# Half of the activations turned by VectorE's 32 x 32 blocks instead of by TensorE, in a one-core hybrid decoder step

## The chip, the cores and the metric

The kernel runs on one core of a Trainium2 chip. The metric is device time in microseconds of one execution, the median of several runs. TensorE (PE) does matmuls and, by an identity matrix, transposes; VectorE (DVE) and ScalarE (ACT) work on data elementwise; GpSimd (POOL) does small copies; SyncE (SP) issues DMAs. POOL and ACT can issue DMAs too, each on a queue of its own.

## The reference

One layer of a decoder, for a prompt of 256 tokens and 8 x 4 sample tokens that share the weights. Each token's row x of 2048 features goes through one wide projection, a gated short convolution (A), a gated DeltaNet (B), a merge with sigmoid gates, an output projection with layer norm, and a feed-forward part with a second layer norm:

```python
proj = x @ w_in
gB, gC, h, q, k, v, z, b_logit, a_logit, m_a, m_b = jnp.split(proj, split_points, axis=-1)
conv_out, new_conv_a = causal_depthwise_conv(gC * h, conv_a_buf, conv_a_w)
y_a = (gB * conv_out) @ w_a_out
qkv, new_gdn_buf = causal_depthwise_conv(jnp.concatenate([q, k, v], -1), gdn_buf, gdn_conv_w)
...
o, S = gated_delta_rule(qh, kh, vh, g, beta, S0)
...
y_b = o @ w_b_out
merged = jax.nn.sigmoid(m_a) * y_a + jax.nn.sigmoid(m_b) * y_b
x = layer_norm(ALPHA * x + merged @ w_o, ln1_g, ln1_b)
x = layer_norm(ALPHA * x + jnp.square(jax.nn.relu(x @ w_up)) @ w_down, ln2_g, ln2_b)
```

All inputs and outputs are float32. The outputs are both token sets, the convolution histories and the delta-rule states.

## The kernel before, in words

**Data layout.** Features lie on partitions and tokens along the free axis: `xh` and `xl` are [128, 16, 288], sixteen feature tiles by 256 prompt and 32 sample tokens. Every float32 operand is split in two: `xh` is x rounded to the matmul format, `xl` the rest, and each weight block likewise into `hi` (a cast on ACT, line 188) and `lo` (a subtraction on DVE, line 143). A product is then three matmuls: hi by xh, hi by xl (line 220) and lo by xh (line 222).

**Blocks.** All weights are cut into blocks of 512 KB, kept in a list `blocks`. One loop runs over them; the order of its statements is the order of the work on each engine, since the program is scheduled by hand. In step i it does the splits of a block two or three ahead, the evacuations that are due (`due`), the matmuls of block i, and the load of block i+6 or i+7 (`load`, SP's queue). `raw`, `hi` and `lo` have four buffers each, so a load waits until the `lo` subtraction of the block four earlier has read the buffer. A block has 24 matmuls of 288 columns; `fill` is a list of small jobs that are slipped into PE's stream, one after each lo matmul (line 223).

**The first eight blocks.** Blocks 0 to 3 need only the first eight feature tiles of x (two tiles each, 512 columns of the k and q projections). Blocks 4 and 5 need feature tiles 8 to 11, blocks 6 and 7 tiles 12 to 15.

**How x gets there.** `xr[i]` (i = 0 to 3) receives 512 features of the 256 prompt tokens, tokens on partitions, rows of 2 KB, and `xs4` the sample tokens. PE turns each 128 x 128 piece (line 942 for the prompt, line 926 for the sample); ACT casts the result from PSUM into `xh`, DVE subtracts to `xl`. For i = 0 this is done ahead of the loop and inside block 0; for i = 1, 2, 3 `x_fill(i)` puts nine transposes (eight and one) into `fill` in blocks 1, 3 and 5.

**Other early loads.** `later_loads` issues `xr[3]`, its sample part and then seven small loads on SP: the convolution histories and weights (`hwr`, `har`) and the norm parameters (`lnr`). PE turns these in block 6 (`hist_tiles`, `hist_tiles2`, lines 968 to 977). The four entries of `rest` load the constants `cf` and `cfe`, the 16 columns of w_in for beta and the decay (`wbar`), and `ci` and `arow`; they are issued at the ends of blocks 2 to 5. `gates`, a generator that runs from block 8 on, copies `wbar` (line 992), adds `xh` and `xl`, and multiplies them (line 1001, in block 13).

**Start of SP's queue.** x tile 0 and the weights of block 0 in pieces, block 1, `xr[1]`, its sample part, blocks 2 and 3, `xr[2]`, its sample part, block 4, then `later_loads`, then block 5.

Of the kernel before, what the change touches and what calls it, by code (L numbers as in the profile page):

```python
# [9 lines left out]
F32 = mybir.dt.float32  # L10
# [6 lines left out]
P = 128  # L17
D = 2048
NP_ = 256
NS = 32  # L20
NT = NP_ + NS
# [85 lines left out]
def hybrid_kernel(ctx: ExitStack, tc: tile.TileContext, A):  # L107
# [31 lines left out]
    act, dve, pe, gps, sp = nc.scalar, nc.vector, nc.tensor, nc.gpsimd, nc.sync  # L139


    def tt(out, a, b, op):
        dve.tensor_tensor(out=out, in0=a, in1=b, op=op)  # L143
# [4 lines left out]
    MUL, ADD, SUB, MIN, MAX = ALU.mult, ALU.add, ALU.subtract, ALU.min, ALU.max  # L148
# [19 lines left out]
    def load(i, steps=(), between=()):  # L168
        if i >= len(blocks):
            return  # L170
        gi, r0, k0, _, _ = blocks[i]
        t = wp.tile([P, KB, GW], F32, tag="raw", name=nm("raw"))
        kb, cols = gi["kb"], gi["cols"]
        dst = t.rearrange("p k c -> p (k c)").rearrange("p (k c) -> p k c", k=kb)
        src = gi["W"][r0:r0 + kb * P, gi["col0"]:gi["col0"] + cols].rearrange("(k p) c -> p k c", p=P)
        k = 0
        for step in steps or (kb,):
            sp.dma_start(dst[:, k:k + step], src[:, k:k + step])
            k += step
            if between:  # L180
                between.pop(0)()
        raw[i] = t
# [67 lines left out]
    xh = xp.tile([P, KT, NT], F32R, tag="XH", name="xh")  # L250
    xl = xp.tile([P, KT, NT], F32R, tag="XL", name="xl")
# [3 lines left out]
    wbar = ao0[:, NL - NE:NL - NE + 16 * KT].rearrange("p (k c) -> p k c", c=16)  # L255
# [609 lines left out]
    tx = tx_cm.__enter__()  # L865
# [6 lines left out]
            pe.matmul(wps.rearrange("p (u c) -> p u c", u=4)[:, 0:u], warm, bmid(warm, u), start=True, stop=True)  # L872

    warm_up(5)
    xr = [tx.tile([P, 2, 512], F32, name=f"xr{i}") for i in range(4)]
    xs4 = tx.tile([P, 512], F32, name="xs4")
    xpr = A["x_prompt"][0].rearrange("(b p) f -> p b f", p=P)
    xsr = A["x_sample"].rearrange("b t (c j p) -> c (b t) j p", j=4, p=P)
    hwr = tx.tile([112, 768], F32, name="hwr")
# [7 lines left out]

    def x_sample_in(c, queue=sp):
        queue.dma_start(xs4[:, c * P:c * P + P], xsr[c])

    def w_first(k, a=0, b=2):
        sp.dma_start(raw[0][:, 2 * k + a:2 * k + b, :],
# [10 lines left out]
    x_sample_in(1)  # L903
    load(2)
    load(3)
    sp.dma_start(xr[2], xpr[:, :, 1024:1536])
    x_sample_in(2)
    gps.memset(epsc[:, 0:1], LN_EPS)
    gps.memset(epsc[:, 1:2], NORM_EPS)
    gps.memset(epsc[:, 2:3], 1.28e-10)  # L910

    def later_loads():
        sp.dma_start(xr[3], xpr[:, :, 1536:2048])
        x_sample_in(3)
        sp.dma_start(hwr[0:96, :], A["state_gdn_conv"][0].rearrange("b j (g c) -> (b j g) c", g=4))
        sp.dma_start(hwr[96:112, :], A["gdn_conv_w"][0].rearrange("j (g c) -> (j g) c", g=4))
        sp.dma_start(har[0:64, :], A["state_conv_a"][0].rearrange("b j (g c) -> (b j g) c", g=4))
        sp.dma_start(har[64:76, :], A["conv_a_w"][0].rearrange("j (g c) -> (j g) c", g=4))
        sp.dma_start(lnr[0:16, :], A["ln1_g"].rearrange("o (k p) -> (o k) p", p=P))
        sp.dma_start(lnr[16:32, :], A["ln1_b"].rearrange("o (k p) -> (o k) p", p=P))  # L920
        sp.dma_start(lnr[32:33, :], A["gdn_norm_w"])


    def x_sample(i):
# [30 lines left out]
    def x_fill(i):  # L955
        def step(u):
            def f():
                turns, out = x_steps(i)[u]()
                for g in turns + out:
                    g()  # L960
            return f
        return step(0), lambda: x_sample(i)(), step(1)

    def hist_tiles():
        g = gtile()
        hv = hw.rearrange("p (g u) c -> p u g c", u=6)
# [19 lines left out]
    def gates(first):  # L986
# [1 line left out]
        xs0 = gd["pool"].tile([P, 12 * NT + KT * 32], F32, tag="S0", name="xf0")  # L988
        xf = (xs0[:, 0:12 * NT].rearrange("p (k t) -> p k t", k=12), gd["pool"].tile([P, 4, NT], F32, tag="b4", name="xf1"))
        wba = xs0[:, 12 * NT:].rearrange("p (k c) -> p k c", k=KT)  # L990
        for u in range(2):
            act.copy(wba[:, :, 16 * u:16 * u + 16], wbar)
        for u in range(4):
            ks = slice(4 * u, 4 * u + 4)
            tt(xf[0][:, ks] if u < 3 else xf[1], xh[:, ks, 0:NT], xl[:, ks, 0:NT], ADD)
            yield
        yield
        gb = gtile()
        for k in range(KT):
# [550 lines left out]
    def side():  # L1550
        first = gdn(0)
        yield from gates(first)
        for G in range(2):
            while cur[0] < mark["kqv", G] + 20 or aux:
                yield
            yield from first if G == 0 else gdn(G)
            if G == 0:
                states_out(0, 24, 3, 27, "kdec", A["new_gdn_conv_prompt"][0, 0], A["new_gdn_conv_sample"][0])
# [45 lines left out]
                     sp.dma_start(arow[:, 0, :], A["a_log"].to_broadcast([P, 8])),  # L1604
                     sp.dma_start(arow[:, 1, :], A["dt_bias"].to_broadcast([P, 8])))]
    load(4)
    later_loads()
    load(5)
    sgen = side()
    gcm = None  # L1610
    for p in range(8):
# [2 lines left out]
    for i in range(len(blocks)):  # L1614
        cur[0] = i
        ahead = AHEAD if i > 9 else 2
        if i == 10:
            split_hi(i + 2)
            split_lo(i + 2)
        if i > 5:  # L1620
            split_hi(i + ahead)
        if i in (1, 3, 5):
            a_, s_, b_ = x_fill(i // 2 + 1)
            fill.extend([idle, a_, s_, b_])
        if i == 6:
            fill.extend([idle, idle, idle, idle, hist_tiles, hist_tiles2])
        if i == 7:
            tx_cm.__exit__(None, None, None)
            gcm = tc.tile_pool(name="gdn", bufs=1)
            gpool = gcm.__enter__()  # L1630
            gd["pool"] = gpool
            gd["w1"] = [gpool.tile([P, 640], F32, tag=f"w1{u}", name=f"w1{u}") for u in range(2)]
            for w in gd["w1"]:
                gps.memset(w[:, 0:3], 0.0)
            gps.memset(stBA, 0.0)
            for G in range(2):
                gd["kq", G] = gpool.tile([P, 4, 4, 2, 64], F32, tag="kq", name=f"kq{G}", bufs=2)
                gd["kqs", G] = gpool.tile([P, 2, 4, 8, 4], F32, tag="kqs", name=f"kqs{G}", bufs=2)
                gd["v", G] = gpool.tile([P, 2, 4, 2, 64], F32, tag="vf", name=f"vf{G}")
                gd["vs", G] = gpool.tile([P, 4, 8, 4], F32, tag="vfs", name=f"vfs{G}")  # L1640
        if i > 7 and sgen:
            if i == mark["merge"]:
                for _ in sgen:
                    pass
                sgen = None
            else:
                next(sgen, None)
                if aux and next(aux[0], aux) is aux:
                    aux.pop(0)
            if i == mark["z"] + 4:  # L1650
                states_out(24, 32, 2, 18, "vf", A["new_conv_a_prompt"][0, 0], A["new_conv_a_sample"][0])
            if i == mark["conv"] + 1:
                gd["ao"] = ap_.tile([P, 2, H, NT], F32, tag="ao", name="ao")
        late = i >= mark["end"] - 1
        if i > 5 and not late:
            split_lo(i + ahead)
        for f in due.pop(i, ()):
            f()
        if late:
            split_lo(i + ahead)  # L1660
        if i == mark["merge"]:
            gcm.__exit__(None, None, None)
            p3 = pool("p3")
            ph["pool"] = p3
            r1 = p3.tile([P, KT, NT], F32R, tag="R1", name="ahl")
            r4 = p3.tile([P, KT, NX], F32R, tag="R4", name="ohl")
            ph["mg"] = p3.tile([P, KT, NX], F32, tag="R3", name="mg")[:, :, 0:NT]

            def halves(key, r, src):
                for q in range(2):  # L1670
                    s = slice(4 * q, 4 * q + 4)
                    s8 = slice(8 + 4 * q, 12 + 4 * q)
                    act.copy(r[:, s, 0:NT], src[:, s, :])
                    tt(r[:, s8, 0:NT], src[:, s, :], r[:, s, 0:NT], SUB)
                ph[key + "h"], ph[key + "l"] = r[:, 0:8, :], r[:, 8:16, :]

            halves("a", r1, gd["ao"][:, 0])
            at(i + 9, lambda: halves("o", r4, gd["ao"][:, 1]))
        if i == mark["down3"]:
            tail_tiles()  # L1680
        if i == mark["down3"] - 60:
            tail_consts()
        if i == mark["end"] - 3:
            sample_sum()
        if i == mark["end"] - 1:
            sample_products()
        matmuls(i)
        if i < 6:
            for u, step in {0: ((1, 2),), 1: ((2, 1), (3, KB))}.get(i, ((i + 2, KB),)):
                split_hi(u, step)  # L1690
                split_lo(u, step)
        if i == 10:
            load(i + 6)
        load(i + ahead + 4)
        if 2 <= i < 6:
            rest[i - 2]()
    for i in sorted(due):
        for f in due[i]:
            f()
# [30 lines left out]
```

## Time and profile before

| | |
|---|---|
| median of 3 runs | 1661.1 us (1660.97 to 1662.16) |
| profiled execution | 1660.64 us, span 1658.7 us |
| granted TensorE clock, mean | 0.999 |
| PE busy | 1650.5 us (100% of the span), 13142 matmuls |
| DVE / ACT / POOL busy | 979.2 / 781.8 / 134.1 us |
| DMA | 280.47 MB, mean 169 GB/s |
| DMA busy share 10 to 20, 20 to 30, 30 to 40 us | 0.93, 1.03, 0.86 |

The span is what the profiler saw of the program; the time is what the run took with what lies around it. Rows of the timeline read: start in us, duration in us, engine, line of the kernel, operation, output<-input, shapes, count, and in brackets how long the engine had been idle and what ended that. SPq and POOLq are DMA issues on those queues. A row with a count above 1 merges neighbours, and its duration runs from the first start to the last end. In the DMA list the last number is the median time from issue to landing.

### The profile page before, as it was taken

The numbers are of one execution on the slowest core, as the hardware profiler recorded it, in microseconds if no ns is written. First come the engines' busy times: TensorE is split into PE (matmuls) and PEld (weight loads), VectorE is DVE, ScalarE is ACT, GpSimd is POOL, SyncE is SP. The second block draws the span as 40 slices with busy tenths as digits, with TensorE's granted clock in tenths as the row PEclk, the third lists the DMA queues.
The fourth block names the chain that finished last, engine by engine and source line by source line (L and its number), as shares of the span: only waits on it lengthen the run. The fifth ranks groups of instructions, "written<-read, shape, count | busy, mean of one in ns | idle before, by whom it ended". The sixth has DMA issues, their size and how long they took to land.

```text
span 1658.7 us, 31399 instructions
## 1 busy us (share of the span) xinstructions
PE 1650.5 (100%) x13142; PEld 1635.6 (99%) x13142; DVE 979.2 (59%) x1299; ACT 781.8 (47%) x1217; POOL 134.1 (8%) x259
## 2 busy tenths in 40 slices
PE   9999999999999999999999999999999999999998
PEld 8999999999999999999999999999999999999997
DVE  6788688767544444457776666444444444444466
ACT  6786756448533333334444455443334433344353
POOL 0142216133000000000000000000000000000011
PEclk9999999999999999999999999999999999999999
DMA  8555457645555555554565555555555555555552
GB/s 272 173 171 169 138 172 203 183 130 176 184 170 165 166 165 166 165 166 154 167 218 165 166 165 166 165 165 166 165 166 165 166 165 166 165 165 166 179 164 97
DMA packets 273251, 280.47 MB, mean 169 GB/s; under 512 B 13727, under 2 KB 267220, under 8 KB 272848
## 3 DMA queue, kind: packets, MB, share of 16 engines
q1 hardware_dynamic: 269334, 266.33, 51.5%
q0 software_dynamic: 3632, 12.08, 2.6%
q8 instruction: 103, 1.69, 0.4%
q14 instruction: 38, 0.31, 0.0%
q10 hardware_dynamic: 144, 0.07, 0.0%
HBM read 270.95 MB, written 7.48 MB: 168 GB/s over the span
## 4 chain that ended last, share of the span: by engine, by line
PE 98%; DVE 1%; ACT 1%; DMA 0%; issue 0%; SPq 0%; ACTq 0%
PE acc L220 62%; PE acc L222 31%; PE acc L725 1%; PE g L1297 0%; PE g L1469 0%; PE g L1489 0%; PE g L1492 0%; PE g L1288 0%; DMA xr<-in_x_prompt_dram 0%; PE g L1189 0%; PE g L1447 0%; DVE lo L143 0%; PE g L1481 0%; PE g L942 0%; DVE w L146 0%
## 5 line engine op out<-in xcount | busy, mean ns | idle before, releaser
L143 DVE TENSOR_TENSOR lo<-raw,hi 128x1024 fp32r<-128x1024 f32 (+1 forms) x503 | 607.4, 1210 | 582.1 <-ACT hi L188 579.2
L188 ACT CAST hi<-raw 128x1024 fp32r<-128x1024 f32 (+1 forms) x499 | 519.2, 1043 | 738.5 <-PE acc L220 654.9
L220 PE MATMUL acc<-xh,hi 128*128 128x288 f32 x1408 | 398.2, 298 | 0.3 <-ACT xh L931 0.2
L220 PE MATMUL acc<-xl,hi 128*128 128x288 f32 x1408 | 394.1, 295 | 0.1
L222 PE MATMUL acc<-xh,lo 128*128 128x288 f32 x1408 | 302.7, 296 | 0.3 <-DVE lo L143 0.3
L220 PE MATMUL acc<-dl,hi 128*128 128x288 f32 (+1 forms) x1024 | 287.7, 295 | 0.0
L220 PE MATMUL acc<-dh,hi 128*128 128x288 f32 (+1 forms) x1024 | 287.7, 296 | 0.0
L220 PE MATMUL acc<-hl,hi 128*128 128x288 f32 x992 | 277.8, 295 | 0.0
L220 PE MATMUL acc<-hh,hi 128*128 128x288 f32 x992 | 277.5, 294 | 0.0
L220 PEld LDWEIGHTS acc<-xh,hi 128*128 128x128 f32 x1408 | 264.5, 188 | 3.1 <-issue 1.1
L220 PEld LDWEIGHTS acc<-xl,hi 128*128 128x128 f32 x1408 | 264.4, 188 | 1.1 <-DVE xl L143 0.3
L222 PEld LDWEIGHTS acc<-xh,lo 128*128 128x128 f32 x1408 | 226.0, 188 | 0.7 <-DVE lo L143 0.7
L222 PE MATMUL acc<-dh,lo 128*128 128x288 f32 (+1 forms) x1024 | 219.9, 296 | 0.0
L222 PE MATMUL acc<-hh,lo 128*128 128x288 f32 x992 | 213.3, 296 | 0.0
L220 PEld LDWEIGHTS acc<-dh,hi 128*128 128x128 f32 x1024 | 193.3, 189 | 0.1
L220 PEld LDWEIGHTS acc<-dl,hi 128*128 128x128 f32 x1024 | 192.9, 188 | 0.1
L220 PEld LDWEIGHTS acc<-hh,hi 128*128 128x128 f32 x992 | 186.4, 188 | 0.4 <-issue 0.4
L220 PEld LDWEIGHTS acc<-hl,hi 128*128 128x128 f32 x992 | 186.2, 188 | 0.0
L222 PEld LDWEIGHTS acc<-dh,lo 128*128 128x128 f32 x1024 | 164.6, 188 | 0.0
L222 PEld LDWEIGHTS acc<-hh,lo 128*128 128x128 f32 x992 | 159.0, 188 | 0.0
L220 PE MATMUL acc<-mh,hi 128*128 128x288 f32 x256 | 71.9, 295 | 0.0
L220 PE MATMUL acc<-ml,hi 128*128 128x288 f32 x256 | 71.7, 295 | 0.0
(419 smaller groups left out, 1481.9 us busy)
## 6 DMA issues: line engine op xcount, KB each, us to landing
raw<-in_w_in_dram SPq DMA_DIRECT2D x175, 512.0 KB, 3.5
raw<-in_w_up_dram SPq DMA_DIRECT2D x128, 512.0 KB, 3.6
raw<-in_w_down_dram SPq DMA_DIRECT2D x128, 512.0 KB, 3.6
raw<-in_w_o_dram SPq DMA_DIRECT2D x32, 512.0 KB, 3.6
raw<-in_w_a_out_dram SPq DMA_DIRECT2D x16, 512.0 KB, 4.1
raw<-in_w_b_out_dram SPq DMA_DIRECT2D x16, 512.0 KB, 3.5
S<-in_state_gdn_dram POOLq DMA_DIRECT2D x8, 512.0 KB, 5.5
out_dram<-S POOLq DMA_DIRECT2D x8, 512.0 KB, 4.6
```

The costliest lines, as they stand in the source:

```text
L143: dve.tensor_tensor(out=out, in0=a, in1=b, op=op)
L188: act.copy(his[i][:, k:k + step], raw[i][:, k:k + step])
L220: pe.matmul(o, h[:, k, c], x, start=st and x is xh_, stop=False)
L222: pe.matmul(o, l[:, k, c], xh_, start=False, stop=en)
L725: pe.matmul(out, x[:, kk, c], w[:, k, :], start=False, stop=stop)
```

## The change

- The features 1024 to 2047 of x (feature tiles 8 to 15) are no longer loaded with tokens on partitions and turned by PE. `x_blocks_in(i)` loads them in pieces of 32 tokens by 8 blocks by 32 features into `xb`, so that partition 32q + r holds token r of every 32-token block, with the 32 features of quarter q: 16 DMAs of 32 partitions for each i, rows of 128 bytes. `x_sample_blocks_in` does the same for the sample tokens, 4 DMAs. All are issued on SP.
- `x_blocks(i)` turns them with DVE's 32 x 32 block transpose into `xt_`, from which ACT casts to `xh` and DVE subtracts to `xl`. It stands behind the matmuls of blocks 2 and 4 (for i = 2 and 3), ahead of the splits of blocks 4 and 6. `x_fill` remains for block 1 only.
- The loads of the second half's first set and of the sample stand ahead of block 4's load; the second set stands between block 5's load and block 6's.
- The seven loads of histories and norm parameters go to GpSimd's queue, at the end of loop step 0, behind a one-element write by DVE to each of the three tiles.
- The four `rest` loads move from the ends of blocks 2 to 5 to those of blocks 5 to 8, and the copies of `wbar` in `gates` move behind the four additions.

```diff
-    xr = [tx.tile([P, 2, 512], F32, name=f"xr{i}") for i in range(4)]
-    xs4 = tx.tile([P, 512], F32, name="xs4")
+    xr = [tx.tile([P, 2, 512], F32, name=f"xr{i}") for i in range(2)]
+    xs4 = tx.tile([P, 256], F32, name="xs4")
+    xb = [tx.tile([P, 4, 8, 32], F32, name=f"xb{i}") for i in range(2)]
+    xt_ = [tx.tile([P, 4, 8, 32], F32, name=f"xt{i}") for i in range(2)]
+    xsb, xst = (tx.tile([P, 8, 32], F32, name=n) for n in ("xsb", "xst"))
...
+    def x_blocks_in(i):
+        src = A["x_prompt"][0].rearrange("(b r) (k q f) -> q r k b f", r=32, q=4, f=32)
+        for k in range(4):
+            for q in range(4):
+                sp.dma_start(xb[i - 2][32 * q:32 * q + 32, k], src[q, :, 4 * i + k])
+
+    def x_sample_blocks_in():
+        src = A["x_sample"].rearrange("b t (k q f) -> q (b t) k f", q=4, f=32)
+        for q in range(4):
+            sp.dma_start(xsb[32 * q:32 * q + 32], src[q, :, 8:16])
...
     load(2)
     load(3)
-    sp.dma_start(xr[2], xpr[:, :, 1024:1536])
-    x_sample_in(2)
+    x_blocks_in(2)
+    x_sample_blocks_in()
...
     def later_loads():
-        sp.dma_start(xr[3], xpr[:, :, 1536:2048])
-        x_sample_in(3)
-        sp.dma_start(hwr[0:96, :], A["state_gdn_conv"][0].rearrange("b j (g c) -> (b j g) c", g=4))
...
+        for t in (hwr, har, lnr):
+            dve.memset(t[0:1, 0:1], 0.0)
+        gps.dma_start(hwr[0:96, :], A["state_gdn_conv"][0].rearrange("b j (g c) -> (b j g) c", g=4))
...
+    def x_blocks(i):
+        u = i - 2
+        for k in (0, 2):
+            dve.transpose(out=xt_[u][:, k:k + 2].rearrange("p k b f -> p (k b f)"),
+                          in_=xb[u][:, k:k + 2].rearrange("p k b f -> p (k b f)"))
+        if u == 0:
+            dve.transpose(out=xst.rearrange("p k f -> p (k f)"), in_=xsb.rearrange("p k f -> p (k f)"))
+        for k in (0, 2):
+            ks, xv = slice(4 * i + k, 4 * i + k + 2), xt_[u][:, k:k + 2].rearrange("p k b f -> p k (b f)")
+            act.copy(xh[:, ks, 0:NP_], xv)
+            tt(xl[:, ks, 0:NP_], xv, xh[:, ks, 0:NP_], SUB)
+        ks, xv = slice(4 * i, 4 * i + 4), xst[:, 4 * u:4 * u + 4]
+        act.copy(xh[:, ks, NP_:NT], xv)
+        tt(xl[:, ks, NP_:NT], xv, xh[:, ks, NP_:NT], SUB)
...
     load(4)
-    later_loads()
     load(5)
+    x_blocks_in(3)
...
-        if i in (1, 3, 5):
-            a_, s_, b_ = x_fill(i // 2 + 1)
+        if i == 1:
+            a_, s_, b_ = x_fill(1)
             fill.extend([idle, a_, s_, b_])
...
         matmuls(i)
+        if i in (2, 4):
+            x_blocks(i // 2 + 1)
...
-        if 2 <= i < 6:
-            rest[i - 2]()
+        if i == 0:
+            later_loads()
+        if 5 <= i < 9:
+            rest[i - 5]()
```

More of the change, by code (lines that the diff above doesn't have):

```diff
@@ L912, in later_loads @@
     def later_loads():
-        sp.dma_start(xr[3], xpr[:, :, 1536:2048])
-        x_sample_in(3)
[L915 to L921, printed above, removed]
+        for t in (hwr, har, lnr):
+            dve.memset(t[0:1, 0:1], 0.0)
+        gps.dma_start(hwr[0:96, :], A["state_gdn_conv"][0].rearrange("b j (g c) -> (b j g) c", g=4))
+        gps.dma_start(hwr[96:112, :], A["gdn_conv_w"][0].rearrange("j (g c) -> (j g) c", g=4))
+        gps.dma_start(har[0:64, :], A["state_conv_a"][0].rearrange("b j (g c) -> (b j g) c", g=4))
+        gps.dma_start(har[64:76, :], A["conv_a_w"][0].rearrange("j (g c) -> (j g) c", g=4))
+        gps.dma_start(lnr[0:16, :], A["ln1_g"].rearrange("o (k p) -> (o k) p", p=P))
+        gps.dma_start(lnr[16:32, :], A["ln1_b"].rearrange("o (k p) -> (o k) p", p=P))
+        gps.dma_start(lnr[32:33, :], A["gdn_norm_w"])
     def x_sample(i):
@@ L990, in gates @@
         wba = xs0[:, 12 * NT:].rearrange("p (k c) -> p k c", k=KT)
-        for u in range(2):
-            act.copy(wba[:, :, 16 * u:16 * u + 16], wbar)
         for u in range(4):
@@ L996, in gates @@
             yield
+        for u in range(2):
+            act.copy(wba[:, :, 16 * u:16 * u + 16], wbar)
         yield
```

## The prediction, made before the changed kernel was run

> **What bounds the kernel now.** I read the page's busy times first, then the chain of work that ended last, then what TensorE (PE) waited for in the first 130 us.
>
> ```profile
> span 1658.7 us, 31399 instructions
> PE 1650.5 (100%) x13142; PEld 1635.6 (99%) x13142; DVE 979.2 (59%) x1299; ACT 781.8 (47%) x1217; POOL 134.1 (8%) x259
> PE 98%; DVE 1%; ACT 1%; DMA 0%; issue 0%; SPq 0%; ACTq 0%
> ...
> PE g L942 <- DMA xr<-in_x_prompt_dram: 0.5, 1, 0.5
> PE acc L222 <- DVE lo L143: 0.3, 1, 0.3
> ```
>
> PE is the chain, and after a start of some 10 us it waits for nobody. So a microsecond taken off PE's stream is a microsecond of the span, and a microsecond for which PE is starved near the start is never given back, because nothing later waits. The change has to be judged by PE's row of blocks between 17 and 34 us. Its timeline gives the block borders (first matmul of blocks 3, 4, 5, 6, 7, and the first transposes inside block 5):
>
> ```profile
> 17.53 0.29 PE L220 MATMUL acc<-xh,hi 128*128 128x288 f32 x1
> ...
> 21.69 0.29 PE L220 MATMUL acc<-xh,hi 128*128 128x288 f32 x1
> ...
> 24.88 0.29 PE L220 MATMUL acc<-xh,hi 128*128 128x288 f32 x1
> ...
> 25.67 0.60 PE L942 MATMUL g<-cf,xr 128*128 128x128 f32 x4
> ...
> 29.05 0.30 PE L220 MATMUL acc<-xh,hi 128*128 128x288 f32 x1
> ...
> 33.35 0.29 PE L220 MATMUL acc<-xh,hi 128*128 128x288 f32 x1
> ```
>
> Block 4 has no transposes and takes 24.88 - 21.69 = 3.19 us (24 matmuls of 0.133). Block 3 takes 4.16 and block 5 takes 4.17: each carries nine transposes of x, at 0.97 and 0.98. Block 6 takes 4.30, so the history transposes cost 1.11.
>
> Then the supply: when SyncE (SP) issued, and when ScalarE (ACT) and VectorE (DVE) could split what landed.
>
> ```profile
> 8.27 0.37 SPq L178 DMA_DIRECT2D raw<-in_w_in_dram  x1
> ...
> 13.17 0.52 SPq L917 DMA_DIRECT2D har<-in_state_conv_a_dram  x1
> ...
> 18.07 0.23 SPq L921 DMA_DIRECT2D lnr<-in_gdn_norm_w_dram  x1
> 18.39 0.39 SPq L178 DMA_DIRECT2D raw<-in_w_in_dram  x1
> ...
> 19.29 1.12 SPq L178 DMA_DIRECT2D raw<-in_w_in_dram  x1
> ...
> 16.32 1.06 ACT L188 CAST hi<-raw 128x1024 fp32r<-128x1024 f32 x1 [0.62 <-DMA raw<-in_w_in_dram]
> ...
> 22.45 1.05 ACT L188 CAST hi<-raw 128x1024 fp32r<-128x1024 f32 x1 [1.57 <-DMA raw<-in_w_in_dram]
> 24.25 1.05 ACT L188 CAST hi<-raw 128x1024 fp32r<-128x1024 f32 x1 [0.75 <-DMA raw<-in_w_in_dram]
> ...
> 23.54 1.23 DVE L143 TENSOR_TENSOR lo<-raw,hi 128x1024 fp32r<-128x1024 f32 x1 [1.93 <-ACT hi L188]
> ```
>
> The 8.27 row loads block 4, the 18.39 row block 5, the 19.29 row block 6; the ACT rows are the splits of blocks 4, 5 and 6, and each waited for its DMA. Block 4's split has ended by 17.4, 4.3 us ahead of need. Block 5's ends at 23.5 for a block that starts at 24.88: 1.4 us to spare. A load takes 22.45 - 18.39 = 4.06 us from issue to split, the one right behind it 24.25 - 19.29 = 4.96. The supply near the start is already close to the edge, and SP's queue is what sets it.
>
> **The change part by part.**
>
> *Removed from PE.* Eighteen transposes go: 0.97 + 0.98 = 1.95 us, all on the path. Without any new wait blocks 4, 5, 6 would start at 20.72, 23.91 and 27.10. This is the whole gain there can be.
>
> *SP's queue.* The order of SP before, from the load of block 3 on (DMAHW0 to DMAHW7 are eight completion counters used in turn, so an issue waits until the DMA eight places earlier has landed):
>
> ```order
> L178 DMA raw_124<-in_w_in_dram 128x2x512 [waits DMAHW2_49]
> L906 DMA xr_105<-in_x_prompt_dram 128x2x512 [waits DMAHW3_49]
> L889 DMA xs_107<-in_x_sample_dram 128x1x128 [waits DMAHW4_49]
> L178 DMA raw_148<-in_w_in_dram 128x4x256 [waits DMAHW5_49,DVE_49]
> L913 DMA xr_106<-in_x_prompt_dram 128x2x512 [waits DMAHW6_49]
> ```
>
> Block 4's load, raw_148, was third behind block 3's. In the changed kernel, the last of the block loads of x ahead of block 4 (the first sixteen write xb_106, these four xsb), and what follows:
>
> ```order
> L904 DMA xsb<-in_x_sample_dram 32x8x32 [waits DMAHW3_49]
> L904 DMA xsb<-in_x_sample_dram 32x8x32 [waits DMAHW4_49]
> L904 DMA xsb<-in_x_sample_dram 32x8x32 [waits DMAHW5_49]
> L904 DMA xsb<-in_x_sample_dram 32x8x32 [waits DMAHW6_49]
> L178 DMA raw_170<-in_w_in_dram 128x4x256 [waits DMAHW7_49,DVE_49]
> L178 DMA raw_172<-in_w_in_dram 128x4x256 [waits DMAHW0_49,DVE_49]
> L899 DMA xb_107<-in_x_prompt_dram 32x8x32 [waits DMAHW1_49]
> L899 DMA xb_107<-in_x_prompt_dram 32x8x32 [waits DMAHW2_49]
> ```
>
> Block 4's load (raw_170) now stands behind twenty DMAs of 32 KB, and block 6's behind sixteen more; in between each pays SP's issue and its counter. So the question is p, the time from one such issue to the next. No row shows a 32 x 8 x 32 load. The nearest are the four stores of 32 rows at the end, 1.76 us together or 0.44 each; the bounds are the one-row issue at 18.07 (0.23) and the 96-row one (0.61).
>
> ```profile
> 1643.60 1.76 SPq L794 DMA_DIRECT2D out_dram<-r  x4
> ...
> 10.65 0.61 SPq L915 DMA_DIRECT2D hwr<-in_state_gdn_conv_dram  x1
> ...
> SPq L917 <- DMA raw<-in_w_in_dram: 1.0, 1, 1.0
> ...
> DMA packets 1469, 0.20 MB, mean 205 GB/s; under 512 B 1358, under 2 KB 1467, under 8 KB 1469
> ...
> DMA packets 499, 0.07 MB, mean 71 GB/s; under 512 B 474, under 2 KB 498, under 8 KB 498
> ```
>
> The last two rows are the microseconds 31 to 33, in which a load of 64-byte rows passed: 1469 and 499 packets per us. A block load has 256 packets (of 128 bytes), so the DMA engines need 0.17 to 0.51 us for it. I take p = 0.44, the store row, since it has the same number of partitions and the engines' 0.17 to 0.51 lies mostly below it.
>
> The sum: the eighth block load has DMAHW2, the counter of block 3's load, as L917 had before, which was released at 13.17 (the wait row). Eight more, the four of the sample and then block 4's load follow: 13.17 + 13p = 18.89, where it stood at 8.27. It lands 4.06 later, at 22.95; hi takes 1.05 (24.00), lo starts 0.04 after that and takes 1.23 (25.27). PE wanted block 4 at 20.72. It starts at 24.00, does four hi matmuls in 0.53, waits 0.74 for lo, and does the other twenty in 2.66: 27.93. Block 5 follows without a wait, to 31.12 (its weights: 19.33 + 4.96 = 24.29). Of the second sixteen, the seventh waits for block 4's landing and the eighth for block 5's, 24.29; eight more and block 6's load: 24.29 + 9p = 28.25, landed 32.31, hi 33.36, lo 34.63. PE wanted block 6 at 31.12: it waits 2.24 and again 0.74, and ends at 34.63 + 2.66 + 1.11 = 38.40 against 33.35 before. So the end moves by **23p - 5.07**, at p = 0.44 by **+5.0 us**: gaps of 4.02 and 2.98, less 1.95. From block 7 on loads are ahead again.
>
> The Trainium skill (DMA: Bandwidth & Descriptors, Issuing engines are not separate DMA queues) says that issue time on a sequencer is usually small beside the DMA itself. By that rule p would be the engines' 0.17 and the sum 23 x 0.17 - 5.07 = -1.2; the 0.44 of the store row speaks against it here, and this is the second rival below.
>
> *DVE and ACT.*
>
> ```profile
> 73.99 0.70 DVE L1131 STREAM_TRANSPOSE S<-kq 128x512 f32<-128x512 f32 x1
> ...
> 18.95 0.59 ACT L948 CAST xh<-g 128x512 fp32r<-128x512 f32 x1 [1.58 <-PE g L942]
> ...
> 20.91 0.69 DVE L143 TENSOR_TENSOR xl<-g,xh 128x512 fp32r<-128x512 f32 x1 [0.45 <-ACT xh L948]
> ```
>
> DVE gains four block transposes of 0.70 and one of half that width, under 0.70: at most 3.5 us. The casts (0.59) and subtractions (0.69) stay, reading SBUF where they read PSUM. They are queued ahead of the split of block 4 on both engines, and wait for the block loads: the last of the sample issues at 13.17 + 12p = 18.45; allowing 2.5 us to land (an assumption), x is done on ACT by about 22, before block 4's weights. The second set's last issue is one p ahead of block 6's load, and its 0.70 + 0.59 fits inside that load's 4.06. So zero; if the weights came early, x itself would be the late one by about a microsecond.
>
> *Histories on GpSimd's queue.* They leave SP, whose places 10.65 to 18.39 they held; this is in the sum, as other DMAs take them. On GpSimd (POOL) seven issues, at 1.94 / 2 = 0.97 each by the state loads, start after DVE's three small writes behind the 9.86 row, at about 11.3, and end by 18.1. PE needs them in block 6, which was 31.31 and becomes later. Zero; their 439 KB (112 rows of 768 numbers, 76 of 256, 33 of 128) compete with the block loads for at most 439 KB at 343 GB/s = 1.3 us, and the block loads leave the engines idle part of the time.
>
> ```profile
> 9.86 1.29 DVE L143 TENSOR_TENSOR lo<-raw,hi 128x512 fp32r<-128x512 f32 x2
> ...
> 74.61 1.94 POOL L1099 DMA_DIRECT2D S<-in_state_gdn_dram  x2
> ...
> 20.00:30.00 10.00, 10.00 (x80) 10.00 (x79) 5.95 (x9) 5.89 (x8) 0.00 (x0) 1.00 1.03 343
> ...
> 34.15 1.23 DVE L143 TENSOR_TENSOR lo<-raw,hi 128x1024 fp32r<-128x1024 f32 x1 [2.56 <-ACT hi L188]
> ...
> 57.86 1.05 ACT L188 CAST hi<-raw 128x1024 fp32r<-128x1024 f32 x1 [3.01 <-PE acc L220]
> ```
>
> *Constants three blocks later.* The beta/a columns of w_in are issued behind block 13's load, which needs block 9's split (34.15 + 1.23, now some 5 later: about 40.4); 5 us on, they are there at 46. Their copy on ACT moves to block 12, near 53, where ACT had 3.0 us idle ahead of 57.86. Zero; without that cover PE would wait at the gate matmuls for what is late. The 1 MB that moves away from 21 to 30 us (128 rows of 770, 906 and 256 numbers) helps the loads behind block 6, which have slack anyway.
>
> **The rivals.**
>
> ```profile
> 16.25 0.31 SPq L920 DMA_DIRECT2D lnr<-in_ln_b_dram  x1
> ...
> raw<-in_w_in_dram SPq DMA_DIRECT2D x175, 512.0 KB, 3.5
> ```
>
> *Block loads barely slow the supply* (p 0.28 to 0.36, and loads landing in the page's median 3.5 us instead of 4.06 and 4.96). At p = 0.36 and 4.06 the end moves by +3.2, with faster landing by up to 1.1 (block 4 and block 6 at 0.56 each) less: +0.5 to +3.2, 1661.6 to 1664.3. For: the 16-row issue took 0.31. Against: the store row, and loads that wait behind others land later, not earlier.
>
> *The gain stands.* The DMA engines' pace sets p, not SP. Break-even is 23p = 5.07, p = 0.22; at 0.17 it is -1.2, and the floor is -1.95: 1659.2 to 1659.9. For: 1469 small packets in one microsecond. Against: no DMA issue in the trace is below 0.23, and SP cannot pass its own issue time.
>
> *PE's clock drops in the gaps.* PE would stand still for 3.3 us ahead of block 4 and 2.2 ahead of block 6. The trace has one such place, its end:
>
> ```profile
> 1652.66 0.96 PE L788 MATMUL g<-g 6*128 6x512 f32 x3 [0.34 <-ACT g L785]
> ...
> 1656.00:1657.00 1.00, 0.00 (x0) 0.00 (x0) 0.00 (x0) 0.00 (x0) 0.00 (x0) 0.60 0.94 330
> 1657.00:1658.00 1.00, 0.00 (x0) 0.00 (x0) 0.00 (x0) 0.00 (x0) 0.00 (x0) 0.50 0.01 2
> ```
>
> Some 2.6 us after PE's last matmul the granted clock is on its way to 0.50. At 0.50 a block takes 6.4 instead of 3.2; a stay of about one block per gap adds 1.6 to 3.2, for one or two gaps: 1667.7 to 1672. It decides from gaps of about 3 us on, which the forecast's first one just reaches. The Trainium skill (TensorE: Matmul & The Clock Gate, The HAM clock gate) gives an idle window of about 3.4 us, free-running, before the clock is halved; by it a gap of 3.3 just escapes, one of 4 does not always.
>
> *Small packets are dear.* At the 96-row issue's 0.61, or with engines at 0.51 and gaps between, p = 0.6 and the end moves by +8.7: 1669.8.
>
> **How the numbers follow.** The profiled execution took 1660.64 us for a span of 1658.7; the median of the three runs is 1661.1, 0.5 above. Differences of the span go onto the median: 1661.1 + 5.0 = **1666.1**. Chances: forecast (p 0.37 to 0.52, 1664.5 to 1668.0) 0.55; barely slows 0.13; gain stands 0.05; clock 0.17; dear packets 0.10. The range 1662.6 to 1670.2 leaves out the gain, the low end of the mild case, and the ends of the last two: about 0.18. Within 0.2% is 3.3 us either way, about what a measurement of this kernel can tell from no change; the gain's floor of 1.95 lies inside it. So faster 0.02, same 0.17 (the mild case and most of the gain), slower 0.81.
>
> **What would show it.** Right: in the changed profile SP's block loads about 0.44 apart from 13 us on, block 4's load near 19 and block 6's near 28; PE idle before blocks 4 and 6, released by hi (ACT L188) and then lo (DVE L143), 7 us in all; blocks 3 and 5 at 3.19. The gates and histories show no PE wait. Wrong: block loads under 0.25 apart; PE waiting for xh or xl (the x path) rather than for hi; a granted clock under 1.00 between 20 and 40 us; or a new wait at the gate matmuls after 50 us.

## The result, and the profile after

| | before | changed |
|---|---|---|
| median, same chip | 1662.16 us (1660.97 to 1662.84, 5 runs) | 1669.49 us (1668.61 to 1671.06, 5 runs) |
| ratio of the times | | 1.0048, 95% interval 1.0033 to 1.0062 |
| profiled execution | 1660.64 us, span 1658.7 | 1671.06 us, span 1669.3 |

The change makes the kernel 0.48% slower. The profiled execution was the longest of its five, so the changed kernel was run a second time, unaltered (label e5_again, below): 1669.09 us, and its profiled execution took 1668.65 with a span of 1666.9. I read both.

The page of the changed kernel, first execution: busy time, and the chain that ended last by engine.

```profile
span 1669.3 us, 31430 instructions
PE 1654.2 (99%) x13124; PEld 1638.2 (98%) x13124; DVE 982.0 (59%) x1307; ACT 782.4 (47%) x1217; POOL 137.7 (8%) x266
PE 96%; DMA 1%; DVE 1%; SPq 1%; ACT 1%; issue 0%; ACTq 0%
```

The eighteen transposes are gone (13142 less 13124), and SP's queue and the DMAs, which had no share of the chain, now have 1% each. PE's timeline says where. First execution: first matmul of blocks 3, 4, 6 and 7, and the first lo matmuls of 4 and 6 (start, length; in brackets the idle time ahead and what ended it).

```profile
19.62 0.29 PE L220 MATMUL acc<-xh,hi 128*128 128x288 f32 x1
...
26.89 0.40 PE L220 MATMUL acc<-xh,hi 128*128 128x288 f32 x1 [3.94 <-ACT hi L188]
28.15 0.85 PE L222 MATMUL acc<-xh,lo 128*128 128x288 f32 x2 [0.47 <-DVE lo L143]
36.92 0.40 PE L220 MATMUL acc<-xh,hi 128*128 128x288 f32 x1 [1.22 <-ACT hi L188]
...
43.59 0.29 PE L220 MATMUL acc<-xh,hi 128*128 128x288 f32 x1
```

Second execution: blocks 4, 6 and 7.

```profile
26.08 0.61 PE L220 MATMUL acc<-xh,hi 128*128 128x288 f32 x1 [5.04 <-ACT hi L188]
...
36.06 0.40 PE L220 MATMUL acc<-xh,hi 128*128 128x288 f32 x1 [0.56 <-ACT hi L188]
37.32 0.53 PE L222 MATMUL acc<-xh,lo 128*128 128x288 f32 x2 [0.47 <-DVE lo L143]
...
41.19 0.29 PE L220 MATMUL acc<-xh,hi 128*128 128x288 f32 x1
```

PE waits for `hi` ahead of blocks 4 and 6 and then for `lo`: the places and the releasers that the forecast named (only in block 4 of the second execution is there no wait for `lo`). The gap ahead of block 4 is longer in the second execution, yet block 6 starts at nearly the same place. Block 7 started at 33.35 before; from its start to the end of the span before has 1658.7 - 33.35 = 1625.35 us, the changed kernel 1625.7 twice. So all but 0.35 us of the loss is made before block 7, and the start of block 7 tells the time:

| kernel | block 7 starts | span | rest |
|---|---|---|---|
| before | 33.35 | 1658.7 | 1625.35 |
| changed, first and second | 43.59, 41.19 | 1669.3, 1666.9 | 1625.7, 1625.7 |
| no block loads (e1) | 32.40 | 1658.3 | 1625.9 |
| moves alone (e6) | 34.20 | 1659.7 | 1625.5 |

The supply, second execution: SP's queue (start, length). The L904 loads are the sample's; the L178 loads are blocks 4 and 5 (one row) and block 6 with five behind it. The rows at 13.77 and 26.52, from narrower stretches, begin at the eighth block load of each set.

```profile
6.41 12.36 SPq L899 DMA_DIRECT2D xb<-in_x_prompt_dram  x16
18.81 1.93 SPq L904 DMA_DIRECT2D xsb<-in_x_sample_dram  x4
20.86 0.94 SPq L178 DMA_DIRECT2D raw<-in_w_in_dram  x2
21.85 8.93 SPq L899 DMA_DIRECT2D xb<-in_x_prompt_dram  x16
30.88 8.26 SPq L178 DMA_DIRECT2D raw<-in_w_in_dram  x6
...
13.77 0.31 SPq L899 DMA_DIRECT2D xb<-in_x_prompt_dram  x1
...
26.52 0.81 SPq L899 DMA_DIRECT2D xb<-in_x_prompt_dram  x2
```

Block 4's load is issued at 20.86 (8.27 before), and block 4 starts 5.22 later; block 6's at 30.88 (19.29 before), and block 6 starts 5.18 later. The four sample loads take 1.93, 0.49 each from start to start. The DMA engines are not the limit there; two microseconds in which little but block loads passed (busy shares of PE, PEld, DVE, ACT and POOL, then granted clock, DMA share, GB/s):

```profile
28.00:29.00 1.00, 1.00 (x6) 1.00 (x6) 1.00 (x2) 0.00 (x0) 0.00 (x0) 0.50 0.44 67
29.00:30.00 1.00, 1.00 (x6) 1.00 (x6) 0.53 (x1) 0.43 (x1) 0.00 (x0) 0.50 0.42 65
```

One 32 KB load per 0.49 us is 67 GB/s, what the row shows, with the DMA engines 0.44 busy: about 0.21 us of their time per load. SP's issue sets the pace. The Trainium skill (DMA: Bandwidth & Descriptors, Issuing engines are not separate DMA queues) calls the issue time usually small relative to the DMA. For one load the trace agrees (0.45 to issue, 3.2 us from issue to landing in the median of the 32 prompt loads); for a row of loads it does not, 0.49 against 0.21 of the DMA engines' time, and the measurement decides.

The same rows show a granted clock of 0.50. It is the second thing that differs from the forecast, and the experiments say what it costs.

### The profile page after: what moved, and what is told of

Read it like the earlier page. It is cut to its first block, busy times and chain, and to the rows that moved or that the text cites. A ratio compares the mean times of both kernels' runs of the same rounds, so it can differ in the third digit from the quotient of the medians.

```text
span 1669.3 us, 31430 instructions
## 1 busy us (share of the span) xinstructions
PE 1654.2 (99%) x13124; PEld 1638.2 (98%) x13124; DVE 982.0 (59%) x1307; ACT 782.4 (47%) x1217; POOL 137.7 (8%) x266
## 4 chain that ended last, share of the span: by engine, by line
PE 96%; DMA 1%; DVE 1%; SPq 1%; ACT 1%; issue 0%; ACTq 0%
PE acc L220 61%; PE acc L222 31%; DMA raw<-in_w_in_dram 1%; PE acc L725 1%; SPq L899 0%; PE g L1327 0%; PE g L1499 0%; PE g L1519 0%; PE g L1522 0%; DVE lo L143 0%; PE g L1318 0%; PE g L1219 0%; PE g L1477 0%; PE g L1511 0%; DVE w L146 0%
```

## The experiments

**Without the block loads (e1_noblocks).** 1661.06 us (1659.83 to 1662.71, 11 runs) beside 1662.34; ratio 0.9994, 0.9985 to 1.0003.

```diff
-        for k in range(4):
-            for q in range(4):
-                sp.dma_start(xb[i - 2][32 * q:32 * q + 32, k], src[q, :, 4 * i + k])
+        gps.memset(xb[i - 2], 0.0)
-        for q in range(4):
-            sp.dma_start(xsb[32 * q:32 * q + 32], src[q, :, 8:16])
+        gps.memset(xsb, 0.0)
```

> The changed kernel with the 36 block loads of x left out (the tiles are set to zero by GpSimd instead, so the second half of x is zero). Theory A (SP's issues of the block loads delay the weights of blocks 4 and 6, and the gaps that this makes in PE's stream drop the clock): block 4's load is issued by about 9 us, no PE gap before blocks 4 and 6, clock at 1.00 from 15 us on, 1.95 us below before: about 1660.2. Rival B (the transposes by VectorE and the casts behind them come too late): the gaps of 4.1 and 1.4 us stay, about 1669. Rival C (the histories on GpSimd's queue or the later constants cost time): some us above 1660 remain, with a PE wait after 40 us.

```profile
7.12 0.44 PE L954 MATMUL g<-cf,xr 128*128 128x128 f32 x2 [1.40 <-DMA xr<-in_x_prompt_dram]
...
32.40 0.29 PE L220 MATMUL acc<-xh,hi 128*128 128x288 f32 x1
```

No gap is left at blocks 4 and 6, and DVE's transposes, the casts and everything that moved are still there. So the loss belongs to the loads. (This kernel leaves the second half of x at zero.) What is left is the gain of the transposes: block 7 starts 0.95 earlier than before although PE waited 1.40 for `xr` at the start where before waited 0.53. With the same start it would be 1.8, near the 1.95 of the forecast. In the timed runs it does not stand clear of no change.

**The moves alone (e6_moves).** The kernel before, with the histories (one of the seven loads is shown), the constants and the `wba` copies moved as in the change: 1661.80 us (1661.06 to 1663.60, 11 runs) beside 1662.67; ratio 1.0000, 0.9991 to 1.0009.

```diff
-        sp.dma_start(lnr[32:33, :], A["gdn_norm_w"])
+        gps.dma_start(lnr[32:33, :], A["gdn_norm_w"])
...
-        if 2 <= i < 6:
-            rest[i - 2]()
+        if i == 0:
+            histories()
+        if 5 <= i < 9:
+            rest[i - 5]()
```

> The kernel before with only the moves of the change: histories on GpSimd's queue, constants for the gates three blocks later, the two wba copies later; TensorE's turns of x and its loads stay as they were. Forecast's pricing (these parts cost nothing): 1661.5 to 1663, ratio 1.000 within 0.001. Rival (the later constants or the histories hold something up): 1663.5 or more, with a wait on hw, w or the gates that the kernel before does not have.

Met, and PE waits at no new place; its wait for `xr` at the start is 1.41, as in e1, but the medians show no loss by it. Pricing these parts at zero was right.

**Each block load cut in two (e4_twice).** 72 issues of 16 KB for 36 of 32 KB, same bytes: 1687.90 us (1687.36 to 1688.65, 4 runs); ratio 1.0155, 1.0141 to 1.0169.

```diff
-                sp.dma_start(xb[i - 2][32 * q:32 * q + 32, k], src[q, :, 4 * i + k])
+                for c in range(2):
+                    sp.dma_start(xb[i - 2][32 * q:32 * q + 32, k, 4 * c:4 * c + 4],
+                                 src[q, :, 4 * i + k, 4 * c:4 * c + 4])
```

> The changed kernel with every block load cut in two (72 issues of 16 KB; same packets, same bytes). Theory A: 0.49 us per added issue, 20 more ahead of block 4's load and 16 more ahead of block 6's, so block 4 starts about 10 us later and block 6 about 18 us later than in the changed kernel: about 17 us more, 1685 to 1688. Rival D (packets): no more than 1 us above the changed kernel, 1670.

What PE waited for (us in total, times, longest), SP's sample loads and second set, and a microsecond inside the latter:

```profile
PE acc L220 <- ACT hi L188: 20.7, 2, 12.5
...
26.10 3.75 SPq L907 DMA_DIRECT2D xsb<-in_x_sample_dram  x8
...
30.96 16.32 SPq L900 DMA_DIRECT2D xb<-in_x_prompt_dram  x32
47.38 8.17 SPq L178 DMA_DIRECT2D raw<-in_w_in_dram  x6
...
36.00:37.00 1.00, 1.00 (x4) 0.87 (x4) 0.62 (x2) 0.42 (x1) 0.00 (x0) 0.50 0.21 32
```

The time is as expected. Eight sample loads take 3.75 us, 0.47 from start to start, where four of twice the size were 0.49 apart, and the DMA engines are only 0.21 busy. The price is per issue, not per byte. Block 4 starts at 34.87 and block 6 at 52.45, 8.8 and 16.4 us after the second execution's and not the 10 and 18 expected. Of the 1687.90 - 1669.49 = 18.4 us between the medians, then, not all is issues: block 6's load is issued 47.38 - 30.88 = 16.5 later, and most of the rest is block 6 at half clock, 59.39 - 52.45 = 6.94 long against 5.13.

**The clock kept up (e2_warm).** Sixteen dummy bf16 matmuls ahead of block 4 and six ahead of block 6, so that PE works in the gaps: 1670.06 us (1669.03 to 1671.32, 5 runs); ratio 1.0048, 1.0035 to 1.0062.

```diff
+        if i in (4, 6):
+            w4 = gtile()
+            for _ in range(16 if i == 4 else 6):
+                pe.matmul(w4.rearrange("p (u c) -> p u c", u=4), warm, bmid(warm, 4), start=True, stop=True)
```

> The changed kernel with 16 matmuls of the bf16 warm-up tile (about 3.5 us) put into PE's stream ahead of block 4 and 6 (about 1.3 us) ahead of block 6, where PE stands idle. Theory A: the gaps stay (the weights come no sooner), but the granted clock stays at 1.00 behind them; two half-speed stretches of 3.4 us at about 1.5 to 1.7 us each go: 3 to 3.4 us below the changed kernel, about 1666. If the clock is not caused by these gaps: the same as the changed kernel or up to 0.5 us more, 1669 to 1670.

A microsecond inside its block 4 (PE, granted clock, DMA share, GB/s), its issue of block 6's load, and the starts of blocks 6 and 7:

```profile
29.00:30.00 1.00, 1.00 (x10) 1.00 0.43 67
...
31.38 8.38 SPq L178 DMA_DIRECT2D raw<-in_w_in_dram  x6
...
36.76 0.40 PE L220 MATMUL acc<-xh,hi 128*128 128x288 f32 x1 [1.59 <-ACT hi L188]
...
41.89 0.29 PE L220 MATMUL acc<-xh,hi 128*128 128x288 f32 x1
```

In its profile the clock stayed at 1.00 and PE made ten matmuls in the microsecond where the changed kernel made six, but the time did not fall. That expectation missed, and the rows say why: block 6 starts 5.38 after its load's issue at 31.38, so what block 4 gains is waited away ahead of block 6. Its block 7 starts at 41.89, later than the 41.19 of the second execution, which ran block 4 at half clock. The halved clock costs something only in block 6: 43.59 - 36.92 = 6.67 in the first execution against 41.19 - 36.06 = 5.13 in the second, 1.5 us in the one execution and nothing in the other.

**The changed kernel again (e5_again).** 1669.09 us (1668.22 to 1669.71, 5 runs) beside 1662.67; ratio 1.0043, 1.0030 to 1.0055.

> The changed kernel itself, unaltered, to stand beside the three below on one chip. Its first profiled run was the longest of its five (1671.06 against a median of 1669.49). Expected: 1668.5 to 1670.5, block 4 at 26 to 27 us and block 6 at 36 to 37.5 us from the start of the span. If the start of the first blocks and the half-speed stretches vary between runs but block 6 stands at the same place, it is SP's queue and not what PE did before that sets it.

Met: start and clock differ from the first execution, block 6 stands 0.9 us from it (36.06 and 36.92), and its load's issue 1.0 (30.88 and 31.89).

**Weights ahead of the first set (e8_order).** 1670.91 us (1670.06 to 1671.74, 5 runs); ratio 1.0054, 1.0041 to 1.0066.

```diff
-    x_blocks_in(2)
-    x_sample_blocks_in()
...
     load(4)
     load(5)
+    x_sample_blocks_in()
+    x_blocks_in(2)
     x_blocks_in(3)
```

> The changed kernel with SP's order altered only: the weight loads of blocks 4 and 5 go ahead of the first 20 block loads; the load of block 6 stays behind all 36. Theory A (what ends last is SP reaching block 6's load near 32 us, whatever the gap at block 4 was): block 4 starts 1 to 3 us sooner (24 to 26 us), its wait for lo goes, the gap at block 6 grows by as much, block 6 at 36 to 37.5 us as before and the time 1668 to 1670.5. Theory B (the two gaps add, as the forecast summed them): the gap at block 4 shrinks by 1 to 3 us and the time with it, 1666 to 1668.

```profile
ACT xh L986 <- DVE xt L980: 13.8, 4, 6.3
...
32.43 8.25 SPq L178 DMA_DIRECT2D raw<-in_w_in_dram  x6
...
28.75 0.61 PE L220 MATMUL acc<-xh,hi 128*128 128x288 f32 x1 [6.81 <-ACT hi L188]
37.60 0.41 PE L220 MATMUL acc<-xh,hi 128*128 128x288 f32 x1 [0.38 <-ACT hi L188]
```

The time is 0.4 us above theory A's range and far above theory B's. Both theories missed block 4: it came later, not earlier, because now x is late, and the casts of x stand ahead of block 4's split in ACT's queue. The test itself still decides: block 4 starts 2.67 later than in the second execution, block 6 only 1.54 later, as much as the issue of its load (32.43 against 30.88). The gaps do not add. Block 6 follows SP, whatever the gap at block 4 was.

**First set on GpSimd's queue (e3_split).** 20 loads there behind a DVE write, the second set on SP: 1665.07 us (1663.55 to 1666.19, 11 runs); ratio 1.0016, 1.0007 to 1.0025.

```diff
-    x_blocks_in(2)
-    x_sample_blocks_in()
...
+    dve.memset(xb[0][0:1, 0, 0, 0:1], 0.0)
+    x_blocks_in(2, gps)
+    x_sample_blocks_in(gps)
```

> The changed kernel with the first sixteen block loads and the four of the sample issued on GpSimd's queue (from about 6 us, behind a one-element write by VectorE, ahead of the histories); the second sixteen stay on SP, between the loads of blocks 5 and 6. Same packets, same transposes. Theory A: block 4's load leaves SP near 8.3 us, block 5's near 11, block 6's near 20, no gap of PE, 1.95 us below before: 1660 to 1661. Rival D (the 128-byte packets themselves load the DMA engines so much that weights land late): gaps before block 4 and 6 of a microsecond or more stay, above 1664.

```profile
19.31 1.19 POOL L904 DMA_DIRECT2D xsb<-in_x_sample_dram  x2 [0.19 <-issue]
...
22.77 0.45 DVE L983 STREAM_TRANSPOSE xst<-xsb 128x256 f32<-128x256 f32 x1 [0.46 <-DMA xsb<-in_x_sample_dram]
...
23.45 1.99 ACT L188 CAST hi<-raw 128x1024 fp32r<-128x1024 f32 x2
...
24.54 0.40 PE L220 MATMUL acc<-xh,hi 128*128 128x288 f32 x1 [3.09 <-ACT hi L188]
```

More than half of the loss goes, with block 6's gap. A gap of 3.09 us stays at block 4, a miss: GpSimd needs 0.6 us for an issue and waited 2.4 us for landings between them, its last ended at 20.5, and block 4's split waited behind the casts of x. The time lies in rival D's range, but its cause is not D's: the split (23.45) follows those casts without waiting for a DMA, so the weights were there, and block 6 has no gap.

**The same without the DVE write (e7_early).** The 20 loads start at 1.5 us (the cut below is against the kernel of e3): 1663.26 us (1662.17 to 1664.55, 11 runs); ratio 1.0007, 0.9998 to 1.0016.

```diff
+    x_blocks_in(2, gps)
+    x_sample_blocks_in(gps)
     x_first(0, 128)
...
-    dve.memset(xb[0][0:1, 0, 0, 0:1], 0.0)
-    x_blocks_in(2, gps)
-    x_sample_blocks_in(gps)
```

> The changed kernel with the first 16 block loads and the 4 of the sample on GpSimd's queue from the start of the program, with no wait ahead of them, and the other 16 on SP between the loads of block 5 and block 6. Theory (what costs is only that block loads stand ahead of weight loads in SP's queue and come late): 20 issues of 0.6 us end near 15 us, x is turned before block 4 wants it, no gap at block 4 and none at block 6: 1660.5 to 1662, as without the loads. Rival (the small packets themselves crowd the first weight and x loads): the wait for xr near 6 us grows by 1 us or more and the time is 1663 or above.

```profile
7.37 0.57 PE L957 MATMUL g<-cf,xr 128*128 128x128 f32 x2 [1.30 <-DMA xr<-in_x_prompt_dram]
...
24.03 0.40 PE L220 MATMUL acc<-xh,hi 128*128 128x288 f32 x1 [0.61 <-ACT hi L188]
```

The gap at block 4 shrinks to 0.61 and the time to within what can be told from no change, though 1 us short of the expectation and at the rival's figure. `xr` lands late, but the wait is no longer than the 1.40 of the kernel without block loads, so it does not show the crowding of the rival. What this execution has and that one lacks is a half-speed stretch at the start, six matmuls a microsecond where e1 made ten (PE, granted clock, DMA share, GB/s):

```profile
9.00:10.00 1.00, 1.00 (x6) 0.50 1.06 299
```

**Turning cut in halves (e9_halves).** The split queues, the sample first, and x turned in two steps, so that block 4's split waits only for tiles 8 and 9: 1663.48 us (1662.80 to 1664.33, 11 runs) beside 1661.64; ratio 1.0010, 1.0001 to 1.0019.

```diff
-        if i in (2, 4):
-            x_blocks(i // 2 + 1)
+        if i in (2, 3, 4, 5):
+            x_blocks(i // 2 + 1, 2 * (i % 2))
```

> The kernel with the split queues (first 16 block loads and the sample's 4 on GpSimd's queue behind a DVE write near 5.5 us, second 16 on SP between the loads of block 5 and 6), with two more edits: the sample's four loads go first, and the turning of x by DVE is cut in two, so that ahead of block 4's split ACT and DVE only hold what block 4 needs (tiles 8 and 9 and the sample), and tiles 10 and 11 come behind block 3's matmuls. In the split kernel PE waited 3.09 us at block 4 because the last of the 20 GpSimd issues (0.6 us each) landed near 22.3 us. Here the twelfth is enough: 5.9 + 12 x 0.65 = 13.7, landed by 17. Theory (x and weights then both come before PE wants them, near 21.4 us): no gap at block 4 nor 6, no lo wait there, 1660.5 to 1662, as without the loads. Rival (GpSimd's issues wait for landings, as some of the split kernel's did by 1 us): a gap of 1 to 2 us stays at block 4, 1662.5 to 1664.

```profile
7.50 0.46 PE L955 MATMUL g<-cf,xr 128*128 128x128 f32 x2 [1.80 <-DMA xr<-in_x_prompt_dram]
31.16 0.40 PE L220 MATMUL acc<-xh,hi 128*128 128x288 f32 x1 [0.89 <-ACT hi L188]
...
25.92 10.32 SPq L178 DMA_DIRECT2D raw<-in_w_in_dram  x6
```

Block 4's gap goes as the theory says, but the time is in the rival's range. What is left is block 6, its load at 25.92 behind the sixteen loads that stayed on SP, and a late start: 1.80 for `xr`, with a half-speed stretch behind it (granted clock 0.50 from 8 to 11 us).

**Block 6's load ahead of the second set (e10_between).** 1664.04 us (1663.11 to 1666.06, 11 runs) beside 1662.51; ratio 1.0012, 1.0003 to 1.0021.

```diff
         load(i + ahead + 4)
+        if i < 2:
+            x_blocks_in(3, sp, (2 * i, 2 * i + 1))
```

> The halves kernel with two edits: SP issues block 6's load first, then eight loads of the second set, block 7's load, then the other eight; and the sample's four loads on GpSimd's queue wait for the same DVE write as the rest (in the halves kernel they went at 2.9 us and PE waited 1.80 us for xr near 6 us). Theory: block 6's load is then issued near 18.5 us, when its buffer comes free, and not at 25.9, so the 0.89 + 0.47 + 0.32 us that PE waited in blocks 6 and 7 go, and x is still in time: 1660.5 to 1662, as the kernel without block loads. Rival (the early load of x, not the late weights, costs what is left): the wait for xr stays above 1.3 us with a half-speed stretch behind it, and the time stays at 1662.5 to 1664.

```profile
25.90 0.40 PE L220 MATMUL acc<-xh,hi 128*128 128x288 f32 x1 [0.46 <-ACT xh L984]
26.62 0.40 PE L220 MATMUL acc<-xl,hi 128*128 128x288 f32 x1 [0.33 <-DVE xl L143]
33.28 0.40 PE L220 MATMUL acc<-xh,hi 128*128 128x288 f32 x1 [0.16 <-ACT xh L984]
34.01 0.40 PE L220 MATMUL acc<-xl,hi 128*128 128x288 f32 x1 [0.32 <-DVE xl L143]
...
9.00:10.00 1.00, 1.00 (x6) 1.00 (x5) 0.66 (x2) 0.14 (x1) 1.00 (x3) 1.00 1.03 352
```

The time missed again, at the upper end of the rival's range, though the wait for `xr` is 0.99 and not above 1.3. The wait for `hi` at block 6 is gone, and x itself is late instead: 1.27 us in four small waits. More weighs at the start, between 8 and 11 us, where PE makes six matmuls a microsecond, the rate of the halved clock, though the rows give 1.00. Why is open. No version beat the kernel before, and the kernel without the loads (0.9994, up to 1.0003) leaves little to be won. Whether fewer and larger loads of the same blocks would pay was not tried.

## Why the prediction was right, step by step

The forecast was 1666.1 in a range of 1662.6 to 1670.2, slower at 0.81; the medians are 1669.49 and 1669.09. The sign, the cause and the places were right, and the size was 3.0 to 3.4 us short: the medians lie above the band of the forecast itself (1664.5 to 1668.0), in the part of the range that was there for the rivals. Of this, 1.1 and 1.6 are the base, since the kernel before stood at 1662.16 and 1662.67 beside them and not at 1661.1. The loss is 7.3 and 6.4 against the forecast 5.0.

**The whole gain, 1.95 us.** Measured 1.8 between e1 and e6, whose starts are alike (waits for `xr` of 1.40 and 1.41): 34.20 - 32.40.

**SP's queue.** The eighth block load of each set did wait, for block 3's load and then block 5's, and the rest ran on SP's issue time. The term that was mis-sized is 13p + 9p, by the pace and by one issue that took long. In the second execution:

| step | forecast | measured |
|---|---|---|
| eighth block load issued | 13.17 | 13.77 |
| the next 13, each | 0.44 | 0.49, and one 1.24; on average (20.86 - 13.77) / 13 = 0.55 |
| block 4's load issued, block 4 starts | 18.89, 24.00 | 20.86, 26.08 |
| eighth of the second set | 24.29 | 26.52 |
| the next 9, each | 0.44 | (30.88 - 26.52) / 9 = 0.48 |
| block 6's load issued, block 6 starts | 28.25, 33.36 | 30.88, 36.06 |
| block 7 starts | 38.40 | 41.19 |

The long issue is a block load of the first set, in the second execution of the changed kernel; the other row is the last of the four stores from which the forecast took 0.44, in the kernel before:

```profile
17.08 1.19 SPq L899 DMA_DIRECT2D xb<-in_x_prompt_dram  x1
...
1644.94 0.42 SPq L794 DMA_DIRECT2D out_dram<-r  x1
```

Block 6's load is 2.63 late: 0.60 from the first counter, 1.37 from the first 13 steps, 0.26 from block 5's landing (5.66 after block 4's issue, not 5.40), 9 x 0.044 = 0.40 from the pace again. Of the 1.37 the long issue makes 1.24 - 0.49 = 0.75 and the pace the other 0.62. The first execution has such an issue too, of 1.47; what holds it the profile does not show. Block 7 is 2.79 late, which makes 1668.5 of the profiled 1660.64 and 7.84; the execution took 1668.65. The stores of the row with 0.44 do start (1644.94 - 1643.60) / 3 = 0.45 apart, so the row was read about rightly; but issues of another shape were taken for these, which are 0.45 long and 0.49 apart, and no term allowed for an issue that is held up. With p = 0.49 alone the forecast's own formula gives +6.2, 1667.3.

**DVE, ACT, histories, constants.** Zero was right: e6 for the moves, e1 for the turning. The assumption that x is ready before block 4's weights held in the changed kernel only because these were late; in e3 and e8, where they came earlier, x was the late one. The forecast had put that at about a microsecond. It was 3.09 in e3, and 6.81 in e8, where its own loads also came later.

**Gaps.** The forecast's formula takes the end from block 6's load, and its words then read it as the sum of two gaps, 4.02 and 2.98, with 0.74 for `lo` in each. The second execution has 5.04, 0.56 and 0.47, the first 3.94, 0.47, 1.22 and 0.47. That two executions divide the idle time so differently and put block 6 at nearly the same place shows which of the two holds: the end is set by SP's arrival at block 6's load, and a longer or shorter gap at block 4 changes nothing (e8, e2).

**The rivals.** *Barely slow* and *the gain stands* fell with p at 0.49. *Small packets are dear* has a time near the one measured, 1669.8, but its p of 0.6 is too high, and the packets were not the cause: the DMA engines were 0.44 busy. *PE's clock drops* came true as an event, at the gap of 3.94 and again after one of 1.22 and 0.47; a granted clock under 1.00 between 20 and 40 us was also a sign of being wrong that the prediction named. The time is in this rival's range (1667.7 to 1672) too, but the price is not the one it gave: the slow block 4 costs nothing, and e2, which keeps the clock up, is no faster. Only block 6 at half clock costs time. Why the first execution is 2.4 us longer than the second divides into 0.86 at block 6's start (its load was issued 1.01 later) and 1.54 at half clock in block 6.

## What to carry to other kernels

When many small DMAs are put into a queue, count issues, not bytes, and take the distance between two starts of such issues from the trace: here the 36 loads were 0.49 us apart at 32 KB and 0.47 at 16 KB, and pushed the weight loads behind them past the need of an engine that never waits again. Then ask which load stands last in that queue, since its issue set where the stage ended; the gap and the slow stretch ahead of that point cost nothing here, and shortening them gained nothing. Before moving work off the busiest engine, compare its whole gain (here 1.95 us) with one late load.

## What the runs showed of the hardware

The halved clock came in steps of one length. In the first execution (busy shares of PE, PEld, DVE, ACT and POOL, granted clock, DMA share, GB/s):

```profile
7.00:8.00 1.00, 1.00 (x7) 1.00 (x8) 0.25 (x1) 0.37 (x1) 0.00 (x0) 0.75 1.07 367
10.00:11.00 1.00, 1.00 (x7) 1.00 (x6) 0.01 (x1) 0.37 (x1) 0.00 (x0) 0.55 1.04 391
...
27.00:28.00 1.00, 0.69 (x4) 0.45 (x4) 1.00 (x1) 0.38 (x1) 0.00 (x0) 0.99 0.56 85
28.00:29.00 1.00, 0.85 (x3) 0.85 (x4) 0.40 (x2) 0.66 (x1) 0.00 (x0) 0.50 0.22 34
...
31.00:32.00 1.00, 1.00 (x8) 1.00 (x8) 0.00 (x0) 0.19 (x1) 0.00 (x0) 0.81 0.42 66
38.00:39.00 1.00, 0.82 (x3) 0.82 (x4) 0.73 (x2) 0.36 (x1) 0.00 (x0) 0.61 1.09 354
...
41.00:42.00 1.00, 1.00 (x8) 0.98 (x8) 0.94 (x1) 0.00 (x0) 0.00 (x0) 0.69 0.87 251
```

A clock of 0.50 for a part of the microsecond gives the row's mean, so the stretches run from about 7.50 to 10.90, 27.98 to 31.38 and 38.22 to 41.62: each 3.40 long, and their starts 20.5 and 10.24 apart, six and three such lengths. In the second execution the clock is 0.58 in the microsecond from 25 and 0.51 in that from 31, so one stretch runs from 25.16 to 31.98: 6.82, two lengths. The second and third stretch of the first execution begin after PE has resumed, which fits a clock that looks back over a fixed stretch of time; idle time of 1.22 and 0.47 in one of them came before the third. The length of the idle time alone does not decide: 1.59 and 0.47 in e2 brought no halved clock, and of the waits for `xr` at the start 1.15 in the first execution did and 1.40 in e1 did not. Where the idle time falls in the window may be the reason; no run shows it. The Trainium skill (TensorE: Matmul & The Clock Gate, The HAM clock gate) describes a free-running activity window of about 3.4 us; these rows agree with the window and its length. That PE must stand still for about a whole window, as the prediction took that page, does not hold here.

GpSimd's issues of the same loads took 0.6 us each (two in 1.19 in e3) against SP's 0.49, so as a second queue it is no faster, only another one.
